# A two-layer backbone on one core: prologue order, the place of the scaled input, and a fixed TensorE order through the attention

## The chip, the cores and the metric

The kernel runs on one core of one Trainium2 chip. A core has five engines that run side by side: TensorE (PE in the profile; PEld is its weight load), VectorE (DVE), ScalarE (ACT), GpSimd (POOL) and SyncE (SP), which issues the loads here. The metric is the time of one execution on the device in microseconds (us); lower is better.

## The reference, cut to what matters

The model has two layers over 256 latent tokens of width 2048; layer 0 also reads 256 context tokens. Everything is fp32.

```
mod = silu(c) @ ada_w[l] + ada_b[l];  shift, scale, gate = split(mod, 3)
h   = rmsnorm(x, norm_g[l]) * (1 + scale) + shift            # context tokens: the same with c_ctx
# layer 0
k, v, q, za, glu, zb = split(h @ w_in)
q = rope(rmsnorm(q, q_norm));  k = rope(rmsnorm(k, k_norm))  # per head, 8 query and 2 key heads of 128
attn = softmax(q @ [k, k_ctx]^T * 128**-0.5) @ [v, v_ctx]
conv = silu(layernorm(depthwise_conv31(a * sigmoid(b)) + b_dw))     # a, b = halves of glu
x = x + gate * (concat(attn * silu(za), conv * silu(zb)) @ w_out)
# layer 1
u, v, z = h @ w_in;  x = x + gate * ((gelu(u) * mix(layernorm(gelu(v))) * silu(z)) @ w_out)
out = rmsnorm(x, final_g)
```

## The kernel before, in words

**Weights and products.** Each weight block of 512 KB is a "W job". SP loads it into a ring of 10 buffers (`raw`). ACT rounds it to a high part (`whi`, L361) and POOL or DVE subtracts to get the low part (`wlo`, L364; blocks 30 to 133 go to POOL, the others to DVE); both have rings of four. TensorE then makes each product three times, high by high, high by low and low by high. A job is 24 matmuls of 256 columns (L386 to L389), or 12 of 512 columns for the q projection (L409 to L411). Results gather in PSUM banks called `acc`, of which there are three.

**Scaled input.** The shift and scale of layer 0 come in five groups (2, 2, 4, 4 and 4 blocks of 128 columns) from small matmuls on "A jobs" (`ada`, L317), whose sums are turned and finished by L330 to L344. For each group `make_h` then builds the input: DVE writes `ht` = x · scale · rstd (L453), ACT rounds `ht` + shift to the high part `h` (L456), and DVE makes the low part from `ht` and `h` (L460). Here `ht`, x, rstd and `h` all lie in SBUF. For the context tokens the same is done with the name `hc`.

**Stages of layer 0.** The glu products of a group run while the next group's A jobs are loaded. The key and value products (`kv`) stand between them. `prep_x` calls `make_h` for the next group. Behind the last group follow, in the plan: the query products (`q_part`), the gate products za and zb, and the two halves of the output product. Gate and layer 1's shift and scale come from a different path, on DVE alone: `traw` blocks times the broadcast silu(c) (L274), with the broadcast in `cb` and copied to a PSUM bank `cbp`.

**Attention.** For each of 16 head and token blocks: one matmul of 512 columns gives `S` (L776), DVE takes the row maximum (L779), ACT the exponential (L782) and the scaling (L785), TensorE turns the result (`ptp`, L796), and for each pair of heads multiplies with the values (`O`, L807). The q rows are turned by rotary tables first (`rope`, L709 to L714), and their norm is folded into the exponential's scale. The depthwise convolution runs as 248 DVE operations (L624, L626) beside all that.

**What sets the order.** A plan (a list of jobs and hooks) gives the program order. Steps of the attention and of the convolution wait in side lists, and after each W job some are taken from them by a pace rule. A scheduler then orders every engine's instructions by its own estimate, within the data dependences, and may pull TensorE's instructions ahead of one another. PSUM's eight banks are shared out by tag: `acc` 3, `S` 1 (shared with two sums), the convolution 1, `cbp` 1, and 2 for everything else, tag `m`.

## Time and profile before

| what | value |
|---|---|
| median of 3 runs | 926.71 us (925.51 to 928.1) |
| the profiled execution | 926.46 us, span 924.7 us |
| TensorE | busy 872.9 us, 94% of the span |
| VectorE | busy 659.6 us, 71% |
| ScalarE | busy 457.9 us, 50% |
| GpSimd | busy 258.6 us, 28% |
| HBM read | 235.80 MB |
| mean granted TensorE clock | 0.975 |

The page gives, for each engine, the busy share in 40 slices of about 23 us, then who waited for whom. "Busy" for TensorE counts pipelined matmuls from issue to end, so a busy slice isn't yet a full one; how many matmuls started in a stretch says more. The granted clock is the share of full speed that the throttle gave TensorE.

### The profile page before, as it was taken

To read this page: it belongs to the slowest core of one execution; us is meant where nothing else is said; L and a number is where in the kernel's file an instruction comes from. 1 tells how busy PE (TensorE), PEld (TensorE's weight loads), DVE (VectorE), ACT (ScalarE), POOL (GpSimd) and SP (SyncE) were. 2 spreads that over 40 slices of the span, in tenths; PEclk is the share of its full clock that TensorE was granted. 3 is DMA by queue.
4 is the path that set the end of the run, shared out by engine and by line. 5 is a ranking of instruction groups with operands and counts; after the bars stand their busy time and mean duration, and the time that the engine had idled before them with its cause. 6 is when DMAs were issued, how large, how long until landed. Compare 5 with 4: busy or idle time off the path is not lost.

```text
span 924.7 us, 17928 instructions
## 1 busy us (share of the span) xinstructions
PE 872.9 (94%) x7084; PEld 800.5 (87%) x7084; DVE 659.6 (71%) x1413; ACT 457.9 (50%) x648; POOL 258.6 (28%) x125
## 2 busy tenths in 40 slices
PE   5999999599998689999999899999999999999994
PEld 3798899599887578998999778998899999999994
DVE  2355684978887877895765299998988977554442
ACT  5643242347557668545544544455583544444441
POOL 0000023659875235686777520000000000000000
PEclk9999999799999899999999899999999999999998
DMA  9999999685776332678889579988887788755402
GB/s 355 406 389 352 363 338 365 252 286 173 233 247 217 121 114 91 205 249 298 312 311 342 175 277 410 409 312 304 311 281 225 250 282 281 218 185 174 137 1 91
DMA packets 66864, 239.06 MB, mean 259 GB/s; under 512 B 7502, under 2 KB 7768, under 8 KB 66268
## 3 DMA queue, kind: packets, MB, share of 16 engines
q1 hardware_dynamic: 66780, 237.92, 72.9%
q8 instruction: 55, 0.90, 0.4%
q14 instruction: 29, 0.24, 0.1%
HBM read 235.80 MB, written 2.10 MB: 257 GB/s over the span
## 4 chain that ended last, share of the span: by engine, by line
PE 76%; DVE 10%; DMA 10%; ACT 3%; issue 1%; POOL 0%; SPq 0%; DVEq 0%; POOLq 0%; ACTq 0%
PE acc L386 17%; PE acc L389 16%; PE acc L388 16%; DMA traw<-adat 7%; PE acc L409 4%; PE acc L410 4%; PE acc L411 4%; DVE traw L274 4%; PE ada L317 3%; PE acc L560 2%; PE acc L562 2%; PE acc L564 2%; DVE conv L626 1%; DMA braw<-ada 1%; PE rms L191 1%
## 5 line engine op out<-in xcount | busy, mean ns | idle before, releaser
L361 ACT ACTIVATE whi<-raw 128x1024 fp32r<-128x1024 f32 (+1 forms) x256 | 263.4, 1031 | 285.1 <-PE acc L388 140.4
L364 POOL TENSOR_TENSOR wlo<-raw,whi 128x1024 fp32r<-128x1024 f32 x104 | 250.9, 2425 | 283.3 <-ACT whi L361 145.4
L364 DVE TENSOR_TENSOR wlo<-raw,whi 128x1024 fp32r<-128x1024 f32 (+1 forms) x152 | 176.8, 1165 | 83.3 <-ACT whi L361 81.7
L274 DVE SCALAR_TENSOR_TENSOR traw<-traw,cbp 128x512 f32<-128x512 f32 x256 | 165.3, 682 | 56.0 <-DMA traw<-adat 52.7
L386 PE MATMUL acc<-h,whi 128*128 128x256 f32 x512 | 152.4, 299 | 8.0 <-DVE gaT L532 6.7
L388 PE MATMUL acc<-h,whi 128*128 128x256 f32 x512 | 149.3, 293 | 0.4 <-DVE h L460 0.4
L389 PE MATMUL acc<-h,wlo 128*128 128x256 f32 x512 | 148.0, 290 | 1.6 <-POOL wlo L364 1.6
L388 PE MATMUL acc<-h1l,whi 128*128 128x256 f32 x512 | 145.2, 284 | 0.0
L389 PE MATMUL acc<-h1h,wlo 128*128 128x256 f32 x512 | 145.0, 283 | 0.0
L386 PE MATMUL acc<-h1h,whi 128*128 128x256 f32 x512 | 145.0, 283 | 0.0
L626 DVE SCALAR_TENSOR_TENSOR conv<-gaT,small,conv 128x241 f32<-128x241 f32 (+14 forms) x240 | 114.6, 478 | 5.2
L386 PEld LDWEIGHTS acc<-h,whi 128*128 128x128 f32 x512 | 100.6, 197 | 14.1 <-issue 10.3
L389 PEld LDWEIGHTS acc<-h,wlo 128*128 128x128 f32 x512 | 100.5, 197 | 4.1 <-issue 2.0
L388 PEld LDWEIGHTS acc<-h,whi 128*128 128x128 f32 x512 | 100.7, 197 | 3.5 <-issue 2.6
L388 PEld LDWEIGHTS acc<-h1l,whi 128*128 128x128 f32 x512 | 98.2, 192 | 0.1
L386 PEld LDWEIGHTS acc<-h1h,whi 128*128 128x128 f32 x512 | 98.2, 192 | 0.1
L389 PEld LDWEIGHTS acc<-h1h,wlo 128*128 128x128 f32 x512 | 98.2, 192 | 0.0
L389 PE MATMUL acc<-m1h,wlo 128*128 128x256 f32 x256 | 73.1, 286 | 0.0
L386 PE MATMUL acc<-m1h,whi 128*128 128x256 f32 x256 | 72.4, 283 | 0.0
L388 PE MATMUL acc<-m1l,whi 128*128 128x256 f32 x256 | 72.4, 283 | 0.0
L389 PEld LDWEIGHTS acc<-m1h,wlo 128*128 128x128 f32 x256 | 49.1, 192 | 2.9 <-issue 2.9
L411 PE MATMUL acc<-whi,h1l 128*128 128x512 f32 x128 | 51.1, 400 | 0.0
(235 smaller groups left out, 1649.1 us busy)
## 6 DMA issues: line engine op xcount, KB each, us to landing
traw<-adat SPq DMA_DIRECT2D x128, 512.0 KB, 5.0
raw<-w_out SPq DMA_DIRECT2D x64, 512.0 KB, 4.0
raw<-w_uz SPq DMA_DIRECT2D x64, 512.0 KB, 4.9
araw<-ada SPq DMA_DIRECT2D x56, 512.0 KB, 6.9
raw<-w_gate SPq DMA_DIRECT2D x56, 512.0 KB, 5.1
raw<-w_v SPq DMA_DIRECT2D x32, 512.0 KB, 5.1
raw<-w_q SPq DMA_DIRECT2D x16, 512.0 KB, 4.1
raw<-w_gate SPq DMA_DIRECT2D x16, 256.0 KB, 11.0
```

The source lines that it names most:

```text
L274: nc.vector.scalar_tensor_tensor(out=jb.raw[:, k, :], in0=jb.raw[:, k, :], scalar=1.0, in1=cbq["t"], op0=ALU.mult, op1=ALU.mult, accum_out ...
L317: nc.tensor.matmul(st8["p"][32 * g : 32 * g + 32, :w], ccol[:, kb, :], jb.raw[:, a, q * w : (q + 1) * w], start=kb < 4 // nq, stop=kb >= N ...
L361: nc.scalar.activation(hv, jb.raw, AF.Copy)
L364: eng.tensor_tensor(out=jb.lo.rearrange("p a b -> p (a b)"), in0=jb.raw, in1=hv.bitcast(F32), op=ALU.subtract)
L386: nc.tensor.matmul(o, wh, hh, start=(n == 0 and kt == kts[0] and b == 0), stop=False, skip_group_check=True)
L388: nc.tensor.matmul(o, wh, hl, start=False, stop=False, skip_group_check=True)
L389: nc.tensor.matmul(o, wl, hh, start=False, stop=end, skip_group_check=True)
L409: nc.tensor.matmul(accs[i], hh[:, sl], jb.hi[:, k, :], start=s0, stop=False)
L410: nc.tensor.matmul(accs[i], hh[:, sl], jb.lo[:, k, :], start=False, stop=False)
L411: nc.tensor.matmul(accs[i], hl[:, sl], jb.hi[:, k, :], start=False, stop=s1)
L560: nc.tensor.matmul(o, hh[:, sl], jb.hi[:, k, :], start=kq == kqs[0] and k == 0 and c == 0, stop=False, skip_group_check=True)
L626: nc.vector.scalar_tensor_tensor(out=o, in0=y, scalar=w, in1=o, op0=ALU.mult, op1=ALU.add)
```

## The change

- **Prologue.** The eight blocks of the first shift and scale group are loaded before the first three weight blocks (`lorder`). Those three are split only after the last shift and scale product. The norm's work is cut in four steps (squares of each half with their sums, the reciprocal root, the broadcast), which stand between the A jobs in the plan. TensorE keeps the program's order up to the first `prep_x`. The broadcast of silu(c) (`make_cb`, eight matmuls) moves from the very start to the beginning of group 1.
- **Scaled input.** In layer 0 `ht` lies in a PSUM bank (tag `m`, two buffers) and no longer in SBUF.
- **Attention.** From the query products to the end of layer 0, TensorE keeps the program's order. The attention's steps are taken at high priority. The list of steps is rewritten: one unit is a head's S, the value product of the pair before, and the turn of the head three before. The norm of q is multiplied into the q rows in PSUM by ACT (16 operations) before `rope`, and the maximum is taken negated in one DVE operation instead of two (16 operations less). `rope` writes into its source.

```diff
+    def make_cb():
+        for q in range(4):
+            pb = bank("cb_p")
+            bcast(pb, q, crh, crl, 4)
+            nc.scalar.copy(cb[:, q * 512 : (q + 1) * 512], pb)
...
+    pe = {"on": True, "all": True}
+    def inorder(op, *args, **kw):
+        with tc.issue_after(pe["last"]) if pe["on"] and "last" in pe else nullcontext():
+            i = op(*args, **kw)
+        pe["last"] = i.ins
+    def loose(op, *args, **kw):
+        inorder(op, *args, **kw) if pe["all"] else op(*args, **kw)
...
     def make_h(src_f, rB, shift, scale, hh, hl, kbs, m=8, rP=None, mh=0):
-            t = tmp.tile([128, 2, T], F32, tag="t2", name="ht", bufs=TB)
+            if m == 4:
+                t = bank("ht").rearrange("p (a b) -> p a b", a=2)
+            else:
+                t = tmp.tile([128, 2, T], F32, tag="t2", name="ht", bufs=TB)
...
     def rope_q(i, cg, src):
-        at["rq"][i, cg] = head_rstd(src, 4, "qss", HD ** -0.5)
+        r = head_rstd(src, 4, "qss", HD ** -0.5)
+        for h in range(4):
+            nc.scalar.activation(src[:, h * 128 : (h + 1) * 128], src[:, h * 128 : (h + 1) * 128], AF.Copy, scale=r[:, h : h + 1])
...
     def attn_head(kvh, c, hq):
-        nc.vector.tensor_reduce(out=mx[:, 0:1], in_=S, axis=AX.X, op=ALU.max)
-        nc.vector.tensor_scalar(out=mx[:, 1:2], in0=mx[:, 0:1], scalar1=rq, scalar2=-1.0, op0=ALU.mult, op1=ALU.mult)
+        nc.vector.tensor_reduce(out=mx[:, 1:2], in_=S, axis=AX.X, op=ALU.max, negate=True)
-        nc.scalar.activation(P, S, AF.Exp, bias=mx[:, 1:2], scale=rq, accum_out=mx[:, 2:3])
+        nc.scalar.activation(P, S, AF.Exp, bias=mx[:, 1:2], accum_out=mx[:, 2:3])
...
     def attn_steps():
+        def unit(n):
+            if n < len(todo):
+                attn_head(*todo[n])
+            if n > AD and (n - AD) % 2 == 0:
+                attn_pv(*todo[n - AD - 1])
+            if AD <= n < len(todo) + AD:
+                attn_tr(*todo[n - AD])
...
-    plan = g0[:S0] + [hook(stats0)] + g0[S0:] + [hook(lambda: prep_x(0))]
+    plan = g0[:2]
+    for f, (a, b) in zip(rms_steps(xh, "rx"), ((2, 4), (4, 6), (6, 7), (7, len(g0)))):
+        plan += [hook(lambda f=f: urgent(f))] + g0[a:b]
+    plan += [hook(lambda: prep_x(0)), hook(lambda: pe.update(on=False, all=False))]
...
+        if g == 1:
+            body = [hook(make_cb)] + body
...
-    lorder = [j for j in g0[:-1]] + early + [g0[-1]]
+    lorder = g0 + early
```

**TensorE at the start.** `ada` with `araw` is a product of the first group, `ada` with `braw` one of the second, `cb_p` the broadcast, `rms` and `csum` the norm, `adat` the turn of the sums. Before:

```order
L170 MATMUL cb_p<-crh,sel 128x512 x2
L171 MATMUL cb_p<-crl,sel 128x512 x2
L170 MATMUL cb_p<-crh,sel 128x512
...
L212 MATMUL csum_b<-ident,rs 128x128 x2
L333 MATMUL adat<-ident,adar 128x128 x2
L317 MATMUL ada_374<-braw,ccol 32x128 x16
L386 MATMUL acc<-h_316,whi 128x256 x3
```

And now:

```order
L194 MATMUL ada_155<-araw,ccol 32x128 x8
L194 MATMUL ada_166<-araw,ccol 32x128 x8
L194 MATMUL rms<-sq,onesD 32x256 x8
...
L194 MATMUL ada_166<-araw,ccol 32x128 x8
L194 MATMUL adat<-ident,adar 128x128
L205 MATMUL ada_358<-braw,ccol 32x128 x16
L194 MATMUL acc<-h_300,whi 128x256 x4
```

The broadcast has left the front; a `braw` product still stands ahead of the first weight matmul (`acc`).

**VectorE at the last `prep_x`.** `h_2267` is the last group's input, `hc` the context's, `gaT` and `gbT` clear a bank `acc` of a finished glu product. Before:

```order
L453 SCALAR_TENSOR_TENSOR ht<-xT_71,modv_133,rB_223 128x256 x4
L453 SCALAR_TENSOR_TENSOR ht<-cT_325,modc,rBc 128x256 x4
L274 SCALAR_TENSOR_TENSOR traw,adat<-traw,cbp 128x512 x2
L532 TENSOR_TENSOR kv_sb<-acc,kv_sb 128x2x256
L460 SCALAR_TENSOR_TENSOR h_2267<-ht,modv_133,h_2267 128x256
L274 SCALAR_TENSOR_TENSOR traw,adat<-traw,cbp 128x512 x2
L460 SCALAR_TENSOR_TENSOR h_2267<-ht,modv_133,h_2267 128x256 x3
L460 SCALAR_TENSOR_TENSOR hc<-ht,modc,hc 128x256
L532 TENSOR_TENSOR gaT<-acc,gaT 128x512
```

And now:

```order
L577 TENSOR_TENSOR gaT<-acc,gaT 128x512
L303 SCALAR_TENSOR_TENSOR traw,adat<-traw,cbp 128x512
L504 SCALAR_TENSOR_TENSOR h_2267<-ht,modv_117,h_2267 128x256 x2
L577 TENSOR_TENSOR gbT<-acc,gbT 128x512
L504 SCALAR_TENSOR_TENSOR h_2267<-ht,modv_117,h_2267 128x256 x2
L497 SCALAR_TENSOR_TENSOR ht<-cT_309,modc,rc 128x256 x4
L504 SCALAR_TENSOR_TENSOR hc<-ht,modc,hc 128x256 x2
L303 SCALAR_TENSOR_TENSOR traw,adat<-traw,cbp 128x512 x2
L504 SCALAR_TENSOR_TENSOR hc<-ht,modc,hc 128x256 x2
L577 TENSOR_TENSOR gaT<-acc,gaT 128x512
```

With two banks, the context's `ht` now follows the latent low parts, and the first `gaT` stands ahead of them all.

**TensorE in the heads.** `qtp` turns q rows. Before, at the change from the first to the second half of the heads:

```order
L769 MATMUL qtp<-ident,qr 128x128 x8
L776 MATMUL S<-kT,qT 128x512
L796 MATMUL ptp<-ident,P 128x128 x4
L776 MATMUL acc<-kT,qT 128x512 x2
L386 MATMUL acc<-h_316,whi 128x256
```

And now, between the first two S (here `acc` with `h_1090` is the q product's weight block):

```order
L194 MATMUL S<-kT,qT 128x512
L194 MATMUL acc<-whi,h_1090 128x512
L194 MATMUL acc<-wlo,h_1090 128x512
L194 MATMUL acc<-whi,h_1090 128x512 x2
L194 MATMUL acc<-wlo,h_1090 128x512
...
L194 MATMUL S<-kT,qT 128x512
```

Twelve matmuls of a weight block now stand between the first S, where several S had stood side by side.

More of the change, by code (lines that the diff above doesn't have):

```diff
@@ L44 @@
 L1 = 2
-P2 = 4
 NF = 3
@@ L177, in backbone_kernel @@
     nc.vector.tensor_tensor(out=crl, in0=crow, in1=crh.bitcast(F32), op=ALU.subtract)
-    for q in range(4):
-        pb = bank("cb_p")
-        bcast(pb, q, crh, crl, 4)
-        nc.scalar.copy(cb[:, q * 512 : (q + 1) * 512], pb)
+    def make_cb():
[3 more added lines that the diff above has]
+            nc.scalar.copy(cb[:, q * 512 : (q + 1) * 512], pb)
     q4 = con.tile([128, 128], F32, name="q4")
@@ L188, in colsum @@
     def colsum(p, ones, src, n, tot):
         g = n % 4
-        nc.tensor.matmul(p[32 * g : 32 * g + 32, :T], ones, src, start=n < 4, stop=n >= tot - 4, tile_position=(0, 32 * g))
+        loose(nc.tensor.matmul, p[32 * g : 32 * g + 32, :T], ones, src, start=n < 4, stop=n >= tot - 4, tile_position=(0, 32 * g))
     def colsum_all(p):
-        r = tmp.tile([128, T], F32, tag="adar", name="csum", bufs=1)
+        r = tmp.tile([128, T], F32, tag="adar", name="csum", bufs=2)
         nc.scalar.copy(r, p[:, :T])
@@ L197, in colsum_all, with csum_copy, csum_rs @@
         o = bank("csum_p")
-        nc.tensor.matmul(o[:, :T], q4, r, start=True, stop=True)
+        loose(nc.tensor.matmul, o[:, :T], q4, r, start=True, stop=True)
         return o
-    def colsum_rstd(p):
-        r = tmp.tile([128, T], F32, tag="adar", name="csum", bufs=1)
+    def csum_copy(p):
+        r = tmp.tile([128, T], F32, tag="adar", name="csum", bufs=2)
         nc.scalar.copy(r, p[:, :T])
+        return r
+    def csum_rs(r):
         o = bank("csum_p")
         for c in range(2):
-            nc.tensor.matmul(o[:, c : c + 1], r[:, c * 128 : c * 128 + 128], q4[:, 0:1], start=True, stop=True)
+            loose(nc.tensor.matmul, o[:, c : c + 1], r[:, c * 128 : c * 128 + 128], q4[:, 0:1], start=True, stop=True)
@@ L328, in ada_fin @@
         nq, nb = cw // w, w // 128
-        r = tmp.tile([128, 256], F32, tag="adar", name="adar", bufs=1)
-        nc.scalar.copy(r[:, :w], p[:, :w])
+        r = tmp.tile([128, 256], F32, tag="adar", name="adar", bufs=2)
+        i = nc.scalar.copy(r[:, :w], p[:, :w])
+        if not h0:
+            crit["critA"] = i.ins
         pt = bank("adat")
         for b in range(nb):
-            nc.tensor.transpose(pt[:, b * 128 : (b + 1) * 128], r[:, b * 128 : (b + 1) * 128], ident)
+            loose(nc.tensor.transpose, pt[:, b * 128 : (b + 1) * 128], r[:, b * 128 : (b + 1) * 128], ident)
         kind, k0 = c0 // D, (c0 % D) // 128
@@ L422, in hook, with rms_steps, half @@
         return jb
-    def rms_rB(src_half, name):
-        pr = bank("rms")
-        for i in range(2):
+    def rms_steps(src_half, key):
+        v = {}
+        def half(i):
+            if i == 0:
+                v["p"] = bank("rms")
             sq = s8("sq")
@@ L433, in rms_rB, with rs, fin @@
             for k in range(8):
-                colsum(pr, onesD, sq[:, k, :], i * 8 + k, 16)
-        rB = tmp.tile([128, T], F32, tag="rB", name=name, bufs=2)
-        nc.scalar.copy(rB, colsum_rstd(pr))
-        return rB
+                colsum(v["p"], onesD, sq[:, k, :], i * 8 + k, 16)
+            if i == 1:
+                v["r"] = csum_copy(v["p"])
+        def rs():
+            v["rs"] = csum_rs(v["r"])
+        def fin():
+            st[key] = tmp.tile([128, T], F32, tag="rB", name=key, bufs=2)
+            nc.scalar.copy(st[key], csum_bc(v["rs"]))
+        return [lambda: half(0), lambda: half(1), rs, fin]
     def split_act(src, hi, lo):
@@ L486, in statsc @@
     def statsc():
-        st["rc"] = rms_rB(st["cx"], "rBc")
+        for f in rms_steps(st["cx"], "rc"):
+            f()
     def prep_x(g):
@@ L532, in part @@
             nc.vector.tensor_tensor(out=dst, in0=a, in1=dst if prev is None else prev, op=ALU.add)
-    turns = []
-    def two_steps(first, second):
-        side["attn"].append(first)
-        if turns:
-            side["attn"].append(turns.pop(0))
-        turns.append(second)
     def kv_part(kqs):
@@ L732, in rope_k @@
         r = head_rstd(src, 2, "kss")
-        kr = tmp.tile([128, 2, 128], F32, tag="kr", name="kr", bufs=2)
+        kr = tmp.tile([128, 2, 128], F32, tag="t2", name="kr", bufs=TB)
         for h in range(2):
@@ L1053, in backbone_kernel @@
     o0b = out_part(w_out0, 0, hm, rms_acc("r1"), range(8, 16), True)
-    heads = attn_steps()
-    kv = [[hook(lambda n=n: side["attn"].extend((turns if n == 0 else []) + heads[n]))] for n in range(2)]
-    kv[1].append(hook(lambda: st.__setitem__("q", True)))
+    kv = [[hook(lambda: side["attn"].extend(attn_steps()))], [hook(lambda: st.__setitem__("q", True))]]
     za, (qa, qb) = z_part(0), q_part()
-    segs = [body, qa + kv[0] + za[:4] + qb, kv[1] + za[4:] + [za_ready], z_part(1) + [conv_tail], [need("attn")] + o0a, [need("conv")] + o0b]
+    segs = [body, [hook(lambda: pe.__setitem__("on", True))] + qa + za[:2] + kv[0] + za[2:4] + qb + [hook(lambda: st.__setitem__("rest", 2))], za[4:8] + kv[1] + za[8:] + [za_ready], z_part(1) + [conv_tail], [need("attn")] + o0a, [need("conv")] + o0b]
     for seg, n in zip(segs, EX):
@@ L1105, in backbone_kernel @@
         j.mm()
+        if j is g0[-1]:
+            for x in early:
+                x.split()
         if j.kind == "W":
             for key in ("attn", "conv"):
+                if key == "attn" and st.get("rest"):
+                    st["rest"] -= 1
+                    continue
                 ahead = [n for k, n in deadline.items() if k == key and n > p]
```

108 lines of the change are left out of this document (52 added, 56 removed).

## The prediction

> **What bounds the kernel now.** I read the page's slices and chain first, then TensorE's matmuls by stretch, then the lost stretches in order of time.
>
> ```profile
> PE   5999999599998689999999899999999999999994
> PEclk9999999799999899999999899999999999999998
> PE 76%; DVE 10%; DMA 10%; ACT 3%; issue 1%; POOL 0%; SPq 0%; DVEq 0%; POOLq 0%; ACTq 0%
> ```
>
> TensorE is busy nearly everywhere, and 76% of the chain that ended last is its own. "Busy" is no rate, so I count matmuls:
>
> ```profile
> core 0: us, PE busy (x) PEld busy (x) DVE busy (x) ACT busy (x) POOL busy (x), PEclk, DMA share, GB/s
> 4.00:60.00 56.00, 47.62 (x637) 39.01 (x638) 24.52 (x61) 32.63 (x54) 0.00 (x0) 0.97 1.03 403
> 168.00:192.00 24.00, 14.45 (x84) 13.90 (x83) 21.97 (x35) 6.96 (x9) 14.69 (x6) 0.72 0.66 234
> 228.00:244.00 16.00, 16.00 (x74) 13.24 (x74) 14.30 (x32) 7.20 (x9) 16.00 (x8) 1.00 0.76 263
> 265.50:369.90 104.40, 92.18 (x535) 75.64 (x534) 84.14 (x222) 71.50 (x118) 47.12 (x20) 0.93 0.44 146
> 752.00:768.00 16.00, 16.00 (x136) 16.00 (x135) 12.71 (x23) 6.97 (x8) 0.00 (x0) 1.00 0.84 275
> ```
>
> Layer 1 gives the full rate: 16.00/136 = 0.118 us for a 256-column matmul. The query products give 16.00/74 = 0.216 us for one of 512 columns. At these rates the kernel loses time in few places: the start (loads saturate at 403 GB/s), 168 to 192 us (84 × 0.118 = 9.9 of 24, so 14.1 lost), and the heads, 265.5 to 369.9. Layer 1 is full and the change does not touch it. So I price three places, and a fourth, the query rows, where the change lays new work on a chain.
>
> **The last scaled input (168 to 192 us).**
>
> ```profile
> 172.22 0.58 PE L389 MATMUL acc<-h,wlo 128*128 128x256 f32 x1 [1.57 <-POOL wlo L364]
> 183.19 0.55 PE L386 MATMUL acc<-h,whi 128*128 128x256 f32 x1 [6.68 <-DVE gaT L532]
> 169.81 12.35 POOL L364 TENSOR_TENSOR wlo<-raw,whi 128x1024 fp32r<-128x1024 f32 x5 [6.00 <-ACT whi L361]
> 169.95 2.50 DVE L460 SCALAR_TENSOR_TENSOR h<-ht,modv,h 128x256 fp32r<-128x256 f32 x1
> 172.37 0.67 DVE L274 SCALAR_TENSOR_TENSOR traw<-traw,cbp 128x512 f32<-128x512 f32 x1
> 173.59 6.38 DVE L460 SCALAR_TENSOR_TENSOR h<-ht,modv,h 128x256 fp32r<-128x256 f32 x3
> 179.89 2.56 DVE L460 SCALAR_TENSOR_TENSOR hc<-ht,modc,hc 128x256 fp32r<-128x256 f32 x1
> 182.37 0.68 DVE L532 TENSOR_TENSOR gaT<-acc,gaT 128x512 f32<-128x512 f32 x1
> L453 DVE SCALAR_TENSOR_TENSOR ht<-xT,modv,rB x24: 472/480/486, 26.3 to 616.3; 128x256 f32<-128x256 f32 x24
> ```
>
> Five low-part operations take 2.50 + 6.38 + 2.56 = 11.4 us, where five of this shape take 5 × 0.48 = 2.4 us elsewhere. They stretch exactly while POOL runs five subtractions of 2.4 us back to back. `traw` with one input in PSUM takes its usual 0.67 in the middle of it, and `gaT`, also with one, 0.68: it is operations whose two inputs both lie in SBUF that wait for POOL. `gaT`, which empties the `acc` bank that TensorE needs, is queued behind them, and TensorE stands 6.68 us and then runs at a clock of 0.72 over the stretch.
>
> With `ht` in PSUM, L460 reads one input from SBUF and should not wait. That alone could give back nearly all 14.1 us. But L453, which writes `ht`, still reads x and rstd from SBUF. It never waited before (at most 486 ns), because it ran while POOL was idle. In the new order the context's four `ht` stand behind the latent low parts, since only two banks hold `ht`, and by then ACT has given POOL its high parts. At worst they wait one subtraction each: 4 × (2.50 − 0.48) = 8.1 us, and `gaT` of the third glu job is behind them. The cover is two jobs of 24 × 0.118 = 2.83 us, 5.7 us, from three `acc` banks; the bare stall of 2.4 us with the 1.57 us wait for `wlo` and some half clock behind it leaves about half of the loss. I take **+7**; ends −2 (all four wait, and the clock drops again) and +14.
>
> The Trainium skill ("SBUF — State Buffer", section SBUF) says that VectorE and GpSimd share one pair of ports under an exclusive lock, which a VectorE operation with two SBUF inputs needs for its whole length against a GpSimd operation that reads SBUF. The rows above agree, and no run yet shows `ht` under it. By that rule the four context `ht` all wait when POOL is busy, which is the −2 to +1 end here and the third case below.
>
> **The start.**
>
> ```profile
> 11.92 0.62 PE L171 MATMUL cb_p<-crl,sel 4*128 4x512 f32 x1
> 12.35 0.62 PE L170 MATMUL cb_p<-crh,sel 4*128 4x512 f32 x1
> 23.23 0.64 PE L317 MATMUL ada<-araw,ccol 128*32 128x128 f32 x16 [1.92 <-DMA araw<-ada]
> 25.82 1.94 PE L317 MATMUL ada<-braw,ccol 128*32 128x128 f32 x32 [0.24 <-DMA braw<-ada]
> 27.69 1.01 PE L386 MATMUL acc<-h,whi 128*128 128x256 f32 x3
> ```
>
> The first weight product at 27.69 follows the last `araw` block (23.23) and a `braw` product (25.82). Loading the eight `araw` first brings the last of them about 2 us sooner, but at 403 GB/s `braw` then comes no sooner, and the new order still has a `braw` product ahead of the first `acc`. That allows 27.69 − 25.82 − 1 = 0.9 us at most. The broadcast leaves a place where TensorE waits for loads anyway and goes into group 1, where it does not: eight matmuls at 0.43 (12.35 − 11.92) or, at full clock, 0.216, so 1.7 to 3.4 us, partly in gaps that group 1 still has. I take **−1**; ends −2.5 and +0.9.
>
> **The query rows.** New are 16 scalings on ACT ahead of the rotary tables, on a chain that ends in S.
>
> ```profile
> 245.38 0.28 ACT L720 ACTIVATE sqj<-acc 128x128 f32<-128x128 f32 x1
> 246.45 1.05 ACT L361 ACTIVATE whi<-raw 128x1024 fp32r<-128x1024 f32 x1
> 247.52 1.28 ACT L223 ACT_TABLE_LOAD   x1
> 248.81 0.30 ACT L223 ACTIVATE qss<-qss,epsc 128x4 f32<-128x4 f32 x1
> 249.27 0.57 ACT L629 COPY gaT<-conv 128x512 f32<-128x512 f32 x1
> 257.89 0.41 DVE L714 TENSOR_TENSOR qr<-rp,rp 128x256 f32<-128x256 f32 x1
> 261.20 0.39 ACT L751 COPY kT<-ktp 128x256 f32<-128x256 f32 x1
> ```
>
> Before, the rotated rows came at 258.3, 13 us after the products, with TensorE full on the za jobs meanwhile. Now TensorE cannot go past the turn of the rows. ACT's list from the first square to the last scale is 8 squares at 0.4 with issue (3.2), a table load 1.28, two roots 0.6, four `whi` 4.2, a copy 0.6, eight scales at 0.28 (2.2; the square of the same tile is the nearest row) and two `kT` 0.8: 12.9 us. DVE's six rotary operations of 0.41 with the convolution between them add about 4.5, so 17.4. The cover is four za jobs, 11.3, with turns and first keys of 2.2: 13.5. The stall is 3.9; some of the `whi` may fall behind the scales, so I take **−3**; ends −6 (no cover for the half clock behind it) and 0 (`whi` of one job less, and more weight work ahead). The 16 negations saved on DVE are in the next part.
>
> **The heads (265.5 to 369.9).**
>
> ```profile
> L776 PE MATMUL S<-kT,qT x22: 590/594/1223, 265.5 to 359.8; 128*128 128x512 f32 x22
> 308.45 2.03 PE L776 MATMUL acc<-kT,qT 128*128 128x512 f32 x2 [2.99 <-ACT z0T L601]
> 314.65 1.41 PE L776 MATMUL S<-kT,qT 128*128 128x512 f32 x2 [2.25 <-ACT P L782]
> 320.48 0.60 PE L796 MATMUL ptp<-ident,P 128*128 128x128 f32 x4
> 350.78 0.86 PE S L776 x2
> 352.83 1.73 PE O L807 x8
> L779 DVE TENSOR_REDUCE mx<-S x11: 674/684/692, 269.7 to 360.4; 128x1 f32<-128x512 f32 x11
> L780 DVE TENSOR_SCALAR mx<-mx,qss x16: 196/206/208, 270.7 to 371.8; 128x1 f32<-128x1 f32 x16
> L782 ACT ACTIVATE P<-S,mx,qss x11: 762/777/780, 271.0 to 364.1; 128x512 f32<-128x512 f32 x11
> ```
>
> From the first S to the last, 103.0 us, TensorE before does 65 × 0.216 + 336 × 0.118 of weight work, 15 S of 0.86, twelve turns of four at 0.44 (the chain has `ptp` x4 at 0.11 each), five O of 1.73 and the turn of q, 0.9: 14.0 + 39.6 + 12.9 + 5.3 + 8.7 + 0.9 = 81.4. So 21.6 us are lost, most of it where S waits for its bank (2.99 and 2.25 above, each with a clock of 0.5 for some us behind; 0.93 over the stretch). In the new order the same stretch, first S to last, holds 72 × 0.216 + 312 × 0.118 and 27.8 of attention, 80.1 us of work, spread evenly: a weight block of 12 × 0.216 = 2.6 us between two S. DVE is nearly as loaded: 84.1 busy of 104.4, less 16 × 0.204 = 3.3, so 80.9. With both full to 80 of about 92 us I expect half of the loss to stay, 10 to 12 us: **+11**. Ends: 0 (it only moves) and 103.0 − 82 = +21, where DVE bounds it.
>
> The rest I set at nothing: the in-place rotation and two table loads fewer (2.6 us of ACT, at 50% busy over the span and off the chain) change no wait on TensorE.
>
> **Sum.** −1 + 7 − 3 + 11 = +14, against the profiled execution: 926.46 − 14 = 912.5, say **912** (its span is 924.7, 1.76 lie around it, and it stands 0.25 below the median 926.71).
>
> **The rivals.**
>
> *Both stalls vanish.* L460 and the context's `ht` fall between POOL's operations, and the heads run to DVE's bound: −1 + 13.8 + 21 = 33.8, with the query chain covered, so 892.5. For it: what is taken away is just what the waits name. Against it: DVE at 80.9 of 82 would have no gap, which no stretch of this profile shows.
>
> *The stall only moves.* The four context `ht` take the wait that L460 had (+1), and the heads gain little since DVE and ACT queue as before (+5); −1 and −3 remain: +2, 924.5, within what can be told from no change. For it: the new place of `ht` behind the low parts and POOL's five subtractions. Against it: `gaT` of the first two jobs stands ahead of them now.
>
> *Slower: TensorE's fixed order in the heads.* Before, TensorE could pass an S that had no bank; now it stands there, with everything behind it. One S occupies its bank for 0.86 + 0.69 (maximum) + 0.78 (exponential) = 2.3 us plus queueing on DVE and ACT; the spacing between S is 2.6 + 0.86 + some turns, 3.6 to 4.5 us. If DVE's queue (conv at 0.5, `traw` at 0.7) and ACT's (`whi` at 1.05) add three us, the loop is 5.4 and every head costs 0.9 to 1.8 us more than its work, and half clock behind. It decides from 26 us lost over 15 heads (1.7 each), where the stretch's loss exceeds the present one by more than the other terms give back. At 2.4 each, 36 us, the stretch is 80 + 36 = 116 instead of 103: −13 there, and with +7 −1 −3 (and −1 for the last turns) 926.46 + 11 = 937.5. For it: S already waits twice with freedom. Against it: attention steps now go first on DVE and ACT.
>
> **How the numbers follow.** Chances: forecast 0.50, both vanish 0.17, only moves 0.18, fixed order 0.15. The forecast's own range is 904 to 920 (prep and heads each off by half of their ends). To leave out about 2 in 10, the range reaches to 894 below, short of the second case, and to 929 above, past the third: **894 to 929**. About 0.3%, 2.8 us, can be told from no change by a measurement of this kernel. Faster by more: 0.50 + 0.17 and four tenths of the third case, 0.74; within it 0.10; slower 0.16, the fourth case and a little of the third.
>
> **What would show it.** In the profile after: L460's successor (`h` from `ht`) at about 0.48 us during POOL's subtractions shows the PSUM step right, and context `ht` of 2.4 us there shows the third case. TensorE's first weight matmul between 27 and 29 us bears on the start. An idle of about 4 us ahead of the turn of q or the first S, ended by ACT or DVE, is the query term. The stretch from first S to last should be near 92 us; 82 would be the second case, 103 the third, 116 the fourth, with waits of S for `P` or `mx` at each head. It is wrong altogether if a stage outside these four moves by more than 5 us, above all layer 1.

## The result, and the profile after

The changed kernel takes 920.78 us (median of 8 runs, 916.09 to 924.59) against 928.33 us before (8 runs, 925.11 to 931.57): a ratio of 0.9926, 95% interval 0.9905 to 0.9948. It is faster by 7.5 us, about half of what was forecast. The profiled execution takes 916.09 us (span 914.3), the shortest of its eight, so the two traces differ by 10.4 us.

The slices and the granted clock of the changed kernel, as before in 40 slices:

```profile
PE   4899999999989899999999899999999999999994
PEclk9999999999999899999999799999999999999997
```

Counted from 0, the dip of TensorE at slice 7 (about 160 to 185 us) is gone, and the dip of the clock with it; a new small one is at slice 11, where the q rows are turned, and one is left at slice 13, in the heads. The stretches that the prediction priced, for the changed kernel (the third row is the heads, from first S to last, the fourth the stretch from there to the first output product):

```profile
core 0: us, PE busy (x) PEld busy (x) DVE busy (x) ACT busy (x) POOL busy (x), PEclk, DMA share, GB/s
4.00:60.00 56.00, 43.19 (x578) 34.19 (x582) 18.05 (x51) 28.52 (x48) 0.00 (x0) 0.97 1.02 402
168.00:192.00 24.00, 20.36 (x152) 19.57 (x151) 22.17 (x45) 11.82 (x17) 16.67 (x7) 0.93 0.85 324
263.00:353.90 90.90, 85.50 (x513) 71.32 (x512) 79.21 (x192) 67.21 (x120) 45.42 (x19) 0.96 0.51 163
353.90:405.40 51.50, 50.40 (x401) 49.40 (x400) 44.49 (x108) 25.86 (x32) 35.92 (x15) 1.00 0.68 222
752.00:768.00 16.00, 16.00 (x136) 16.00 (x135) 10.70 (x22) 6.62 (x9) 0.00 (x0) 1.00 0.77 261
```

From 168 to 192 us TensorE now starts 152 matmuls instead of 84. The heads take 90.9 us instead of 104.4. Layer 1 runs at the same 16.00/136. And this row of the kernel before answers the fourth:

```profile
369.40:416.60 47.20, 47.20 (x377) 46.56 (x376) 43.25 (x101) 22.25 (x27) 34.39 (x15) 1.00 0.68 226
```

Behind the last S, up to the first output product, stand 401 matmuls now and stood 377 before: 24 more, one whole weight block.

**The prep stage.** VectorE and GpSimd at the last scaled input of the changed kernel, in order of time (start, duration, line, what):

```profile
173.12 9.79 POOL L395 TENSOR_TENSOR wlo<-raw,whi 128x1024 fp32r<-128x1024 f32 x4 [5.85 <-ACT whi L392]
174.93 0.86 DVE L504 SCALAR_TENSOR_TENSOR h<-ht,modv,h 128x256 fp32r<-128x256 f32 x2
176.31 0.86 DVE L504 SCALAR_TENSOR_TENSOR h<-ht,modv,h 128x256 fp32r<-128x256 f32 x2
177.10 6.49 DVE L497 SCALAR_TENSOR_TENSOR ht<-cT,modc,rc 128x256 f32<-128x256 f32 x4
183.74 0.88 DVE L504 SCALAR_TENSOR_TENSOR hc<-ht,modc,hc 128x256 fp32r<-128x256 f32 x2
186.53 0.68 DVE L577 TENSOR_TENSOR gaT<-acc,gaT 128x512 f32<-128x512 f32 x1
```

L504 (L460 before) reads `ht` from PSUM and takes 0.43 us each beside POOL's subtractions (173.12 to 182.91 us); it no longer waits. The context's `ht` (L497), with both inputs in SBUF, waits in its place: 6.49 us for four that take 4 × 0.48 = 1.9 elsewhere. Behind it stands the `gaT` of the third glu job.

What TensorE waits for, from the waits in the changed kernel's profile (engine, line waited for: us in total, times, longest):

```profile
PE S L194 <- ACT P L815: 5.4, 3, 4.5
PE acc L194 <- DVE gaT L577: 2.0, 1, 2.0
PE acc L194 <- DVE mBl L482: 1.6, 1, 1.6
PE acc L194 <- ACT z0T L637: 1.3, 1, 1.3
PE O L194 <- ACT PT L830: 1.1, 1, 1.1
PE ktp L194 <- ACT kT L787: 1.0, 1, 1.0
```

The wait for `gaT` fell from 6.7 to 2.0. New is one for `mBl`, the low part of the convolution's half of layer 0's last product; those for `z0T` and `kT` stand among the query rows (254 to 258 us), where the kernel before had none, and that for `PT` behind the last S.

### The profile page after: what moved, and what is told of

Read it like the earlier page. It is cut to its first block, busy times and chain, and to the rows that moved or that the text cites. A ratio compares the mean times of both kernels' runs of the same rounds, so it can differ in the third digit from the quotient of the medians.

```text
span 914.3 us, 17929 instructions
## 1 busy us (share of the span) xinstructions
PE 867.0 (95%) x7084; PEld 795.6 (87%) x7084; DVE 650.0 (71%) x1397; ACT 457.8 (50%) x662; POOL 257.4 (28%) x125
## 4 chain that ended last, share of the span: by engine, by line
PE 81%; DMA 10%; DVE 6%; ACT 1%; issue 1%; POOL 0%; SPq 0%; DVEq 0%; POOLq 0%; ACTq 0%
PE acc L194 71%; DMA traw<-adat 6%; PE ada L205 3%; DVE traw L303 2%; PE O L194 2%; PE rms L205 1%; DMA braw<-ada 1%; DVE ht L497 1%; DMA araw<-ada 1%; PE S L194 1%; PE sgu L991 1%; PE ptp L194 1%; DMA xT<-xT 1%; DMA wsT<-wsT 1%; POOL wlo L395 0%
## 5 line engine op out<-in xcount | busy, mean ns | idle before, releaser
L194 PE MATMUL acc<-h,whi 128*128 128x256 f32 x1024 | 193.7, 289 | 4.7 <-DVE gaT L577 2.0
L194 PEld LDWEIGHTS acc<-h,whi 128*128 128x128 f32 x1024 | 161.3, 193 | 11.0 <-ACT whi L392 4.3
L194 PE MATMUL acc<-h,wlo 128*128 128x256 f32 x512 | 145.4, 285 | 0.3 <-POOL wlo L395 0.3
L194 PEld LDWEIGHTS acc<-h,wlo 128*128 128x128 f32 x512 | 98.6, 193 | 1.5 <-issue 0.8
L194 PE MATMUL acc<-whi,h 128*128 128x256 f32 (+1 forms) x256 | 68.0, 345 | 1.3 <-ACT z0T L637 1.3
L194 PEld LDWEIGHTS acc<-whi,h 128*128 128x128 f32 x256 | 44.5, 189 | 8.3 <-ACT z0T L637 1.7
```

What stands on the lines that cost most here:

```text
L194: i = op(*args, **kw)
```

## The experiments

All times are medians beside runs of the kernel before on the same chip (927.7 to 928.7 us); the ratio to it stands with its 95% interval. For every run the trace was cut at the same marks: first weight product, a glu sum late in group 2 counted from 0 (128.8 us in the kernel before; the expectations call it the sum of group 1), the third of the four key and value sums of group 4, first S, last S, first output product of layer 0, first product of layer 1. Durations between marks, in us, from one profiled execution each:

| kernel | time | ratio | start | prep | query | S to S | behind S | output | layer 1 |
|---|---|---|---|---|---|---|---|---|---|
| before | 928.33 | 1 | 101.1 | 82.0 | 54.7 | 103.5 | 47.6 | 112.7 | 395.3 |
| changed | 920.78 | 0.9926 | 104.1 | 74.4 | 57.2 | 90.5 | 51.9 | 112.0 | 396.9 |
| changed, again | 919.39 | 0.9910 [0.9886, 0.9934] | 104.8 | 75.0 | 56.7 | 88.6 | 51.9 | 115.4 | 395.6 |
| before, ht in PSUM | 918.81 | 0.9918 [0.9888, 0.9948] | 100.5 | 75.3 | 55.5 | 98.6 | 47.6 | 115.1 | 396.9 |
| changed, ht in SBUF | 926.87 | 0.9995 [0.9981, 1.0009] | 105.1 | 80.3 | 56.4 | 89.9 | 51.9 | 116.8 | 396.6 |
| changed, old prologue | 916.29 | 0.9883 [0.9856, 0.9909] | 101.0 | 74.3 | 56.7 | 90.5 | 51.9 | 118.7 | 397.4 |
| changed, early broadcast and old loads | 916.56 | 0.9870 [0.9841, 0.9898] | 100.3 | 74.7 | 57.4 | 91.0 | 51.9 | 116.2 | 396.2 |
| changed, free order | 916.71 | 0.9878 [0.9844, 0.9912] | 104.7 | 74.8 | 54.8 | 90.6 | 50.7 | 112.5 | 398.5 |
| old prologue and free order | 910.76 | 0.9815 [0.9782, 0.9849] | 101.1 | 73.8 | 54.8 | 91.0 | 50.7 | 111.5 | 394.8 |

Single stretches scatter from one execution to the next: the two profiles of the same changed kernel differ by 3.4 us in the output products alone. How prep and query rows divide depends on the mark, because VectorE takes these sums with a varying delay. By TensorE's own first key and value product of group 4 (200.24 us before, 196.06 and 197.59 in the two profiles of the changed kernel) prep gains 6.9 and 6.2 us and the query rows lose 1.7 and 1.2.

**The changed kernel once more.**

> The changed kernel once more, unchanged, for a second profile. Its eight times run from 916.1 to 924.6 us with a median of 920.8, and the one profiled took 916.1. Theory 'the profiled execution was a short one': this one takes 919 to 923 us, the stretch from first to last S stays at 90 +- 1 us as in the first profile, and the further 3 to 6 us lie in some other stretch, which the two profiles set side by side will name. Rival 'the terms were sized right and the timing is off': about 916 us again, and a ratio to before below 0.988.

919.39 us, 0.9910 [0.9886, 0.9934]. The time is where the theory had it, but the profile was again a short one (917.39 us), so the 2 to 5 us between the two profiles and the medians were not caught whole. First to last S takes 88.6 us, a little under the 89 to 91 expected; the stretch that differs most is the output products. The forecast had been made against one execution on each side, and the changed kernel's runs spread over 9 us.

**Only the scaled input.** Before plus

```diff
-            t = tmp.tile([128, 2, T], F32, tag="t2", name="ht", bufs=TB)
+            if m == 4:
+                t = bank("ht").rearrange("p (a b) -> p a b", a=2)
+            else:
+                t = tmp.tile([128, 2, T], F32, tag="t2", name="ht", bufs=TB)
```

and, the other way round, the changed kernel without this edit:

> The kernel before with only the scaled input of layer 0 moved to PSUM. Theory (terms add): the low parts of the last prep stage take 0.48 us each beside POOL's subtractions, the context's scaled inputs wait in their place, TensorE's wait of 6.7 us at the glu product shrinks to 2 to 3 us, and the kernel gains 5 to 7 us (ratio 0.9925 to 0.995). Rival (the stall only moves): in the old order more operations stand behind the context's inputs, the wait of 6.7 us stays at 5 or more under another name, ratio 0.998 to 1.002.

> The changed kernel with the scaled input of layer 0 back in SBUF, all else as changed. Theory (terms add): 5 to 7 us slower than the changed kernel, so 925 to 928 us, ratio to before 0.997 to 1.000, low parts of 2.4 us each again at the last prep stage. Rival (the new order of the rest already keeps these operations away from POOL): within 2 us of the changed kernel, ratio 0.992 to 0.995.

918.81 us alone, and 926.87 us without it. The additive theory was borne out both times, in the first run with more than was forecast (8.9 us where 5 to 7 were expected). TensorE's longest wait of this stage, with the edit alone (first row, from 135 to 205 us) and in the changed kernel without it (second, from 135 to 212 us):

```profile
PE acc L386 <- DVE gaT L535: 2.7, 1, 2.7
```

```profile
PE acc L194 <- DVE gaT L574: 8.1, 1, 8.1
```

And the operation that waits, in the changed kernel without it:

```profile
172.67 12.34 POOL L395 TENSOR_TENSOR wlo<-raw,whi 128x1024 fp32r<-128x1024 f32 x5 [6.07 <-ACT whi L392]
176.45 6.38 DVE L501 SCALAR_TENSOR_TENSOR h<-ht,modv,h 128x256 fp32r<-128x256 f32 x3
182.74 2.55 DVE L501 SCALAR_TENSOR_TENSOR hc<-ht,modc,hc 128x256 fp32r<-128x256 f32 x1
```

So the same rows come back with SBUF and go with PSUM. This edit is nearly all of the change's gain: everything else together, 0.9995, is worth nothing that can be told apart from zero. The rest of the study asks why.

**The start.** Five kernels, first with the whole old prologue, then with one part of it undone at a time, last with two. The parts are the old loads (with them the early weight blocks are split ahead of the last shift and scale product again), the early broadcast (`make_cb` at the very front), and the free start:

```diff
-    lorder = g0 + early
+    lorder = [j for j in g0[:-1]] + early + [g0[-1]]
...
-        if g == 1:
-            body = [hook(make_cb)] + body
+    make_cb()
...
-    pe = {"on": True, "all": True}
+    pe = {"on": False, "all": False}
```

> The changed kernel with the whole prologue as before: old load order, broadcast of silu(c) at the front, the norm in one piece, the early weight blocks split ahead of the last shift and scale product, TensorE free to reorder until the query products. Theory of the prediction (the start costs 1): 919 to 920.5 us, 0 to 2 us faster than the changed kernel. Rival (the 5 to 6 us by which the key and value sums of group 0 come later in the changed kernel are not made up): 915 to 917 us, 4 to 6 us faster.

916.29 us, 0.9883: 3 to 4 us faster than the changed kernel, as the rival had it, and the stretch is 101.0 again. The prediction's 1 us was too little.

> The changed kernel with only the eight broadcast matmuls back at the very front. Theory (these eight, at 0.33 us each among full work, are the start's loss): 2 to 3.5 us faster than the changed kernel, 916 to 918 us, nearly as the whole old prologue (916.3). Rival (the load order and TensorE's fixed order are the loss): within 1 us of the changed kernel.

922.47 us, 0.9937 [0.9913, 0.9961], stretch 104.6: the theory fell.

> The changed kernel with TensorE free to reorder in the prologue; load order, late split of the first three weight blocks and late broadcast stay. Theory 'the fixed order is the start's loss': first weight product to the sum of group 1 (104 us in the changed kernel, 101 in the kernel before) falls to 101 to 102, time 2 to 4 us less. Rival 'the loads and the split of the first weight blocks are the loss': stays at 104, within 1 us of the changed kernel.

919.38 us, 0.9915 [0.9889, 0.9940], stretch 104.7: no change.

> The changed kernel with the first three weight blocks loaded ahead of the last shift and scale block and split before its product, as in the kernel before; fixed order and late broadcast stay. Theory 'the loads and the split are the loss': first weight product to the sum of group 1 falls from 104 to 101 to 102 us, time 2 to 4 us less. Rival 'the fixed order is the loss': stays at 104, within 1 us of the changed kernel.

920.93 us, 0.9922 [0.9896, 0.9948], stretch 104.2: no change either. No single part is the loss.

> The changed kernel with two parts of the prologue undone together: the broadcast at the very front, and the first three weight blocks loaded and split as in the kernel before; TensorE's fixed order and the norm in steps stay. No part alone shortened the 104 us from the first weight product to the sum of group 1 (104.6, 104.3, 104.7), all together did (101.0). Theory 'the late broadcast and the late loads each hide the other': 101 to 102 us, and 917 to 918 us in time. Rival 'the fixed order is needed for the loss too': 104 us, 919 us or more.

916.56 us, 0.9870 [0.9841, 0.9898], stretch 100.3: all of it, with the fixed order and the norm's steps still there. The late broadcast and the late loads each hide the other. In the changed kernel the eight broadcast matmuls run between 54.3 and 61.3 us, a stretch in which TensorE waits for nothing; the first two of them:

```profile
54.28 0.49 PE L168 MATMUL cb_p<-crh,sel 4*128 4x512 f32 x1
54.61 0.39 PE L169 MATMUL cb_p<-crl,sel 4*128 4x512 f32 x1
```

With the broadcast alone undone the loss stands earlier, at the first weight blocks. From 25 to 45 us, in the changed kernel, then with the broadcast alone at the front:

```profile
25.00:45.00 20.00, 19.50 (x246) 17.18 (x250) 5.38 (x15) 12.51 (x21) 0.00 (x0) 0.91 1.03 407
```

```profile
25.00:45.00 20.00, 18.92 (x184) 16.80 (x185) 6.63 (x16) 11.24 (x19) 0.00 (x0) 0.75 1.03 407
```

184 matmuls start there instead of 246, at a clock of 0.75 instead of 0.91. From 60 to 90 us, in the changed kernel, then with both undone:

```profile
60.00:90.00 30.00, 29.96 (x422) 25.63 (x414) 15.38 (x30) 11.58 (x21) 0.00 (x0) 1.00 0.83 282
```

```profile
60.00:90.00 30.00, 28.31 (x379) 25.33 (x380) 13.50 (x26) 9.66 (x17) 0.00 (x0) 0.97 0.89 332
```

TensorE is busy throughout in the first, and the loads run at 282 instead of 332 GB/s. The waits of SP's queue from 27 to 132 us, changed kernel and then both undone:

```profile
SPq L117 <- PE ada L205: 32.5, 17, 6.0
```

```profile
SPq L117 <- PE ada L207: 28.3, 15, 5.3
```

That the broadcast costs TensorE's time when TensorE is behind, and that the weights come too late when it isn't, is argued from these rows; that both must be undone is shown. Why the late loads cost nothing more while the broadcast is late stays open.

**The query rows.**

```diff
-        for h in range(4):
-            nc.scalar.activation(src[:, h * 128 : (h + 1) * 128], ..., AF.Copy, scale=r[:, h : h + 1])
+        at["rq"][i, cg] = head_rstd(src, 4, "qss", HD ** -0.5)
...
-        nc.scalar.activation(P, S, AF.Exp, bias=mx[:, 1:2], accum_out=mx[:, 2:3])
+        nc.scalar.activation(P, S, AF.Exp, bias=mx[:, 1:2], scale=rq, accum_out=mx[:, 2:3])
```

> The changed kernel with the norm of q folded into the exponential again (16 ACT scalings less, 16 negations on DVE more), the order as changed. Theory of the prediction (the scalings lie on the path to the turn of q, stall 2 to 3 us): the stretch from the last sum of group 4 to the first S is 1 to 3 us shorter than the changed kernel's 57, the time 0 to 3 us less. Rival (the stretch is set by something else on the way, or the 16 negations cost as much in the heads): within 1 us, or slower.

921.0 us, 0.9932 [0.9909, 0.9956]. The stretch to the first S is 54.1, 2.6 to 3 us shorter, as forecast; S to S and behind it are as in the changed kernel; and in the output products 119.3 us pass instead of 112 to 115. In this profile the gain is there and is given back behind the heads. That pointed to what stands there.

**The convolution.** In the kernel before its last operation starts at 416.4 and the first output product at 416.6. In the changed kernel TensorE is there at 405.4, 11 us sooner, and the convolution's last operation starts at 411.4, only 5 us sooner. The first half of the output products takes the attention and not the convolution. What needs the whole convolution first are the last sums of its norm (`cmean`), which TensorE reaches a few us later. The last convolution operation and these sums, before, then in the changed kernel:

```profile
415.88 0.98 DVE L626 SCALAR_TENSOR_TENSOR conv<-gaT,small,conv 128x242 f32<-128x242 f32 x2
419.59 1.07 PE L191 MATMUL cmean<-gaT,onesC 128*32 128x256 f32 x16
```

```profile
411.37 0.47 DVE L662 SCALAR_TENSOR_TENSOR conv<-gaT,small,conv 128x241 f32<-128x241 f32 x1
412.56 0.63 PE L205 MATMUL cmean<-gaT,onesC 128*32 128x256 f32 x4
```

Before, the sums start 2.7 us behind the convolution's end; in the changed kernel the last four start 0.7 us behind it, as in every profile in which TensorE waits for them (0.6 or 0.7). The slack at this point is used up.

Two kernels leave out the last 23 taps of the last two channel blocks (46 of 248 operations; this part of the convolution is not computed):

```diff
         for n in range(t0, t1):
+            if i >= 6 and n >= 8:
+                continue
             t = TAPS[n]
```

> The kernel before with 46 of the 248 convolution operations left out (of the last two channel blocks only the first 8 of 31 taps are taken), so the convolution ends some 20 us earlier and the heads ahead of it hardly change; part of the convolution is not computed. Theory (in the kernel before the convolution ends just in time, at 416.4 with the first output product at 416.6, and TensorE hardly waits for it): 0 to 2 us faster than the kernel before. Rival (the convolution bounds both kernels alike): 4 us or more faster.

> The same 46 convolution operations left out of the changed kernel. Theory (the heads' gain is partly given back because TensorE now arrives ahead of the convolution): TensorE's waits for the layer norm's sums and for the second input's low part (1.6 to 7 us in the profiles so far) go, 3 to 5 us faster than the changed kernel, and the gap to the kernel before with the same cut grows from 7.5 to 10 us or more. Rival (the heads simply gain no more than 5 us, convolution or not): the gap stays at 7 to 8 us.

The changed kernel gained 5 to 6 us (914.89, 0.9854 [0.9833, 0.9874]), its runs drew together (913.9 to 916.7), the waits for the norm's sums and `mBl` fell to 0.4 and 0.2 us, and the gap between the two kernels grew to 18 us. The kernel before did not gain but lost 5 us (933.14, 1.0051 [1.0031, 1.0071]), which neither theory had. Its rows say what happened, and at the same time what the tail hangs on:

```profile
432.51 0.69 DVE L274 SCALAR_TENSOR_TENSOR traw<-traw,cbp 128x512 f32<-128x512 f32 x1 [4.53 <-DMA traw<-adat]
433.73 2.47 DVE L641 TENSOR_TENSOR gaT<-gaT,csum_p 128x512 f32<-128x512 f32 x4
435.13 1.07 PE L191 MATMUL cvar<-csq,onesC 128*32 128x256 f32 x4 [4.76 <-ACT csq L644]
```

The norm's subtraction (L641) stood in VectorE's queue behind a `traw` product that waited 4.53 us for its load, and TensorE waited 4.76 us for what follows. So the shorter convolution was no clean cut in the kernel before, and how much of the gap of 18 us is the convolution's own can't be said.

```diff
-    ...extend([conv_stats] + [lambda p=p: conv_fin(p) for p in range(4)])
+    ...extend([lambda: urgent(conv_stats)] + [lambda p=p: urgent(lambda: conv_fin(p)) for p in range(4)])
```

> The changed kernel with the convolution's layer norm and its second input taken at high priority, ahead of the gate and layer 1 products (`traw`) in VectorE's queue. Theory (TensorE arrives ahead of the convolution, whose last steps stand behind traw operations that wait for loads): the waits for the norm's sums and the second input's parts fall under 1.5 us, first output product to layer 1's first product at most 112 us (112 to 117 in the profiles of the changed kernel), time 915 to 918 us and a narrower spread than 916 to 925. Rival (the taps themselves, not their tail, come late): within 1 us of the changed kernel, the waits as before.

922.91 us, 0.9930 [0.9905, 0.9954]. The waits did go and the output products took 108.8 us, as expected, but 3 us came back behind the last S (54.9 instead of 51.9) and some more in layer 1 (399.5): high priority for the convolution's tail only moved the loss. That queueing in this tail alone takes the gain is not borne out.

```diff
-PACE = 1.4
+PACE = 2.0
```

> The changed kernel with the old prologue (916.3 us, 2.5 to 3 less than the changed kernel) and one number more: the convolution's steps are taken at a pace of 2.0 instead of 1.4, so they enter the program order sooner. Theory (TensorE waits for the convolution's layer norm behind the heads, and VectorE has room earlier): the last convolution operation 5 to 15 us sooner than 412, waits for the norm's sums and the second input's low part under 2 us, time 911 to 915 us. Rival (VectorE is full and the heads only get later by what the convolution gains): 915 us or more, last S 4 us or more later.

919.25 us, 0.9901 [0.9863, 0.9939] (912.8 to 921.9 over six runs). The last convolution operation came at 407.5, 5 us sooner, and the last S no later (349.2 after 350.4), but the time is no better than that of the old prologue alone. A shift by pace settles nothing.

**The fixed order.** Undone from the query products on:

```diff
-    segs = [body, [hook(lambda: pe.__setitem__("on", True))] + qa + za[:2] + ...
+    segs = [body, qa + za[:2] + ...
```

> The changed kernel with TensorE free to reorder from the query products to the end of layer 0; units, priority and scaled q rows as changed. Theory (the fixed order spreads S between weight blocks and makes the heads' gain): first to last S goes from 90 towards 98 to 103 us, the same stretch to the first output product 4 to 9 us longer, but only 0 to 3 us of it reach the end since TensorE then no longer waits for the convolution; time 919 to 924 us. Rival (the units' order and the priority make the gain, not the fixed order): 90 +- 2 us from first to last S.

916.71 us, 0.9878 [0.9844, 0.9912]: better than expected, and the rival is right on the heads. First to last S takes 90.6 us with TensorE free: the units and their priority make the heads' gain, not the fixed order. Whether it is the order of the units or their priority was not tried apart; the folded kernel has 88.8 us, so the scaled q rows and the saved negations do not make it. What the fixed order costs is 2 us ahead of the first S (54.8 against 56.7 to 57.2), 1.2 behind the last (50.7 and 51.9) and, on average, some in the output products. From 400 to 520 us, in the kernel with the free order (one wait for the convolution; the others of that view belong to layer 1's norm), then in one with the fixed order (the one with the old loads, the worst here):

```profile
PE cmean L205 <- ACT gaT L665: 2.0, 1, 2.0
```

```profile
PE cmean L205 <- ACT gaT L665: 4.4, 1, 4.4
PE acc L194 <- DVE mBl L482: 1.7, 1, 1.7
PE acc L194 <- ACT mBh L481: 0.2, 1, 0.2
```

Ten profiles with the fixed order up to layer 1 (without the two that touch the convolution's work or priority) have 112.0 to 121.4 us there, 116.7 on average; the kernel before and the one with `ht` alone have 112.7 and 115.1. TensorE's waits there for the convolution's norm and second input sum to 1.6 to 7.3 us in the ten, to 1.0 in the kernel before, 2.7 with `ht` alone and 2.0 with the free order. In nine of the ten TensorE stands at the last `cmean` 7.2 or 7.3 us behind its first output product, with the free order not until 14.0 us behind it (the first output product starts at 402.7 there):

```profile
417.09 0.98 DVE L662 SCALAR_TENSOR_TENSOR conv<-gaT,small,conv 128x242 f32<-128x242 f32 x2
418.74 1.07 PE L205 MATMUL cmean<-gaT,onesC 128*32 128x256 f32 x4 [1.95 <-ACT gaT L665]
```

So there the convolution may end 15 us behind the first output product, and TensorE has other work until then.

```diff
-[need("attn")] + o0a
+[need("attn"), hook(lambda: pe.__setitem__("on", False))] + o0a
```

> The changed kernel with TensorE's fixed order ended where the attention ends, ahead of layer 0's output products, instead of at the end of layer 0; prologue, heads and all else as changed. Theory (the fixed order costs nothing in the heads and 3 to 5 us in the output products, where TensorE stands at the second input while that comes late from the convolution): first output product to layer 1's first product 109 to 113 us instead of the 112 to 121 of the nine profiles with fixed order, time 915 to 918 us as with the free order throughout (916.7). Rival (the fixed order costs its 3 us in the query products and heads): 919 to 922 us.

919.18 us, 0.9904 [0.9881, 0.9927], between the two, the output products 113.0. The intervals overlap with both, so it stays open how the 3 us divide between the stretch up to the first output product and the output products.

**Together.**

> The changed kernel with the old prologue and with TensorE free to reorder in the attention: what is left of the change is the scaled input in PSUM, the units, their priority and the scaled q rows. Theory (the old prologue gave 3 to 4 us, the free order 3, and they add): 912 to 915 us. Rival (both only bring TensorE sooner to the convolution): 915.5 to 918 us, as each alone.

910.76 us, 0.9815 [0.9782, 0.9849]: the two add, with a little more than was forecast. The interval lies clear of that of the old prologue alone (0.9856 to 0.9909) and of the changed kernel (0.9905 to 0.9948). This is the fastest version, 17.9 us under the kernel before. TensorE reaches its first output product 14 us ahead of the convolution's last operation here (398.7 and 412.8), and the output products still take only 111.5 us.

> The same with the convolution's layer norm and second input at high priority. Theory (the wait for the convolution is what eats the rest): 909 to 913 us, 2 to 4 us less than without. Rival (the taps come late): within 1 us of the kernel without.

914.74 us, 0.9859 [0.9830, 0.9888], no gain, rather a loss: again 3 us behind the last S (53.7).

> The fastest so far (old prologue, free order: 910.8 us) with the norm of q folded into the exponential again. Theory (with TensorE no longer held up behind the heads, the 2.6 us that the folding saves ahead of the first S are kept): 907.5 to 909.5 us. Rival (S waits for the exponential in the heads, and the 16 negations on VectorE cost as much): 910 to 912.5 us.

914.37 us, 0.9864 [0.9839, 0.9889]: rather slower. With the free order the first S comes at the same place (54.7 after 54.8), so the scaled q rows cost nothing there any more. The last convolution operation starts 160 us behind the first S instead of 156, and the output products take 118.9 instead of 111.5 us; that the 16 negations back on VectorE delay the convolution so is argued, not shown.

## Why the prediction was wrong, step by step

The direction was right and the time lies in the range, but the likeliest value was 14 us of gain where 7.5 came. (The forecast's own range, with prep and heads each off by half of their ends, comes to 904 to 922, not to 920.)

- **The prep stage, +7, was right in mechanism and size.** It takes 74.4 and 75.0 us instead of 82.0, so +7.3 (+6.5 by TensorE's own mark), and the edit alone gave 0.9918 in time (0.9888 to 0.9948, 5 to 10 us). The third case's condition, that the context's `ht` waits for POOL, came true as well (4.6 us beyond their own 1.9, where 8.1 was the bound), but the cover of two jobs held it to 2.0 us of stall on TensorE, 3.4 in the second profile. On the Trainium skill ("SBUF — State Buffer", section SBUF): its rule that a VectorE operation with two SBUF inputs and a GpSimd operation that reads SBUF lock each other out agrees with the rows of the three kernels shown here: L460 and L501 with `ht` in SBUF (2.1 to 2.6 us each), L497 (1.6 each) but not L504 (0.43) with `ht` in PSUM.
- **The start, −1, was mis-sized: it measures −3.4** (104.1 and 104.8 against 101.1), the largest error among the four terms. The step that failed is "partly in gaps that group 1 still has": where the eight matmuls now run, TensorE has no gap, and at 0.33 us each they take an estimated 2.7 us (8 × 0.33). The prediction also credited the new load order with up to 0.9; the first weight product comes 0.2 to 0.3 us sooner (27.49 and 27.35 after 27.69), and the late loads of the first weight blocks that go with it hold the same 3 us when the broadcast is undone.
- **The query rows, −3, measure −2.3** (−1.4 by TensorE's own mark). TensorE waits 2.6 us there, where it waited for nothing before, and the folded kernel has no such wait (54.1 us). So ACT's list is the cause, as the prediction had it, but only 0.3 of the 2.6 is the wait for the q rows; 1.3 is for `z0T` and 1.0 for `kT`, which ACT does too. It takes the fixed order as well, as "Now TensorE cannot go past the turn of the rows" has it: with the free order the stretch is 54.8 us with the scaled rows and 54.7 without.
- **The heads, +11, measure +13.0 and +14.9 from S to S and then −4.3 behind the last S: +9.6.** The step that failed is "the same stretch, first S to last": it ended the account at the last S. The forecast's 72 and 312 matmuls are just what the trace has in that stretch, against 65 and 336 before, so 24 matmuls of weight work had moved behind the mark, where they are counted (401 against 377): 2.8 us at 0.118. Another 1.1 is TensorE's wait for `PT`.
- **"The rest I set at nothing": the output products of layer 0 and layer 1.** The two profiles lose 1.0 us on average in the output products (112.0 and 115.4 against 112.7) and as much in layer 1 (396.9 and 395.6 against 395.3). In the output products TensorE's waits for the convolution's norm and second input grew from 1.0 to 1.6 and 3.2 us, and to as much as 7.3 in other kernels with the fixed order. The prediction gave them no term: it set the bound of VectorE inside the heads (81 of 82 us) and did not ask where TensorE meets the end of VectorE's longest chain. That these waits make the changed kernel's longer executions long is argued from the ten profiles, since no profile of the changed kernel itself is a long one.
- **The baseline.** Both profiles of the changed kernel are among its shortest executions. In them the four terms sum to 11.3 us instead of 14, all stretches to 9 to 10, and the medians differ by 7.5. Where the last 2 us lie is not shown; with the ten profiles' average of the output products the sum would be 6 to 7. The prediction took one execution for the kernel.

Of the rivals, the fixed order's did occur, but not where it was placed: the S loop did not stall at each head (S waits 5.4 us in all, 4.5 of it at one place), and with the free order S waits 6.4. The fixed order costs at the query rows and, probably, at the convolution's norm and half of the output products.

## What to carry to other kernels

When work is pulled ahead on the bounding engine, read which other chain it meets next in its own order and how long before that the chain ends, and price the stretch up to there and not to the last instruction that was moved. Here the norm's sums stood 2.7 us behind the convolution's end before, and 0.7, as near as they ever stood, after. An operation with both inputs in SBUF that runs beside GpSimd is worth moving one input to PSUM, alone, before anything is rearranged: here that was the whole gain that could be told apart. A fixed order on an engine is cheap only where all its operands come early; and parts of a rearrangement that hide one another (late broadcast, late loads) must be undone together before either is cleared.

## What the runs showed of the hardware that was not expected

TensorE's granted clock fell to a half after little waiting. In the changed kernel TensorE waits three times between 172.5 and 175.6 us, the longest for 1.11 us:

```profile
173.09 0.50 PE L194 MATMUL acc<-h,whi 128*128 128x256 f32 x2 [0.23 <-ACT whi L392]
174.70 0.50 PE L194 MATMUL acc<-h,whi 128*128 128x256 f32 x2 [1.11 <-ACT whi L392]
175.56 0.58 PE L194 MATMUL acc<-h,wlo 128*128 128x256 f32 x1 [0.35 <-POOL wlo L395]
187.36 0.47 PE L194 MATMUL acc<-h,whi 128*128 128x256 f32 x2 [1.96 <-DVE gaT L577]
```

and the stretches behind these waits show a clock of 0.50 behind the three short ones and of 1.00 behind the single one of 1.96 us:

```profile
176.00:178.00 2.00, 2.00 (x11) 2.00 (x11) 2.00 (x4) 0.55 (x1) 2.00 (x2) 0.50 1.01 404
187.30:190.80 3.50, 3.44 (x29) 3.48 (x30) 2.62 (x7) 0.37 (x1) 3.50 (x3) 1.00 0.99 337
```

So the length of one wait did not tell whether the clock fell. The spread between executions was not expected either: the changed kernel does the same work in every run and its times lie 9 us apart (916 to 925), while with 46 convolution operations less they lie within 3 us (four runs). That the convolution's end spreads them is suggested by this, not shown.
